# The last feed-forward projection and the final norm, token-major instead of feature-major

## The chip, the cores and the metric

The kernel runs on one core of a Trainium2 chip. The metric is the device time of one execution in microseconds (us), as the median of several runs.

## What is computed

The reference is a decoder trunk of two layers over 512 tokens of 1024 features, all in float32. Each layer mixes tokens in three gated branches (spatial gating, sliding-window attention, gated delta rule), adds the merged result through an output projection, and then adds a SwiGLU feed-forward part. A last RMSNorm follows. What the change touches is the end:

```
x = x + merged @ w_out[layer]
h2 = rmsnorm(x, ffn_norm[layer])
gu = h2 @ w_gate_up[layer]                      # 2 x 2816 columns
x = x + (silu(gu[:, :2816]) * gu[:, 2816:]) @ w_down[layer]
...
out = x * rsqrt(mean(x * x, over features) + 1e-6) * final_norm
```

## The kernel before

**Layout.** Activations are feature-major: a tile holds 128 features on the partitions and all 512 tokens along them, so x is KT = 8 tiles, and the feed-forward activation is KF = 22 tiles. Every matmul is done in three parts, because float32 values are split into a high and a low half (`H` and `L` in the names): high by high, high by low, low by high. In the feature-major projections (`fm_acc`, `fm_tile`) a 128x128 piece of the weight is loaded into TensorE and 512 tokens of an activation stream past it, into one PSUM bank. Some projections are token-major (`tm_group`, among them the z projection `z_proj`): there a 128x128 piece of the activation is loaded, for a chunk of 128 tokens, and 512 columns of weight stream.

**Weights** come through `wload`: one DMA on SP into a staging tile `st` (two buffers), a cast on ScalarE to the high half `wh`, and a subtraction on VectorE to the low half `wl` (three buffers each). These carry a high priority, so they run ahead of the matmuls as buffers allow.

**Order.** A planner (`Issue`) with estimated costs writes the order of TensorE's instructions; streams hand over to each other with `yield`. The other engines and the DMA queues are ordered by the framework's scheduler, by readiness and place in the program. The order on each engine and queue is thus fixed before the run.

**PSUM.** Four banks with the tag `mm` serve the projections, four with the tag `px` the small products.

**Output projection of a layer.** For each m of 8 tiles: 24 matmuls, then the residual tile `xt` is read from DRAM (SP), added on VectorE, written back to `xscr` (SP), and passed to `Norm.add`, which makes the halves `hH` (ScalarE) and `hL` (VectorE) of x times the norm's gain, the square `sq` (ScalarE), and the sum of squares (GpSimd or VectorE). `xt` and `sq` share a pool of five buffers with the tag `rot`.

**Feed-forward part.** 44 tiles of gate and up projection (`wg`), of which the 22 activations are made and split (`aH`, `aL`); then for each m of 8 tiles 22 x 3 = 66 matmuls with `wd`, the residual `xf` and `Norm.add`. In the last layer `Norm.add` squares, sums and multiplies by the final gain. `Norm.finish` then turns the sum of squares into a per-token factor: matmuls with a column of ones, the power -0.5 on GpSimd, a diagonal tile `dg`, a matmul that spreads it over the partitions, and a copy to `rep`. All eight tiles are multiplied by `rep` and written out.

Of the kernel before, what the change touches and what calls it, by code (L numbers as in the profile page):

```python
# [10 lines left out]
F32 = mybir.dt.float32  # L11
# [25 lines left out]
LAT = 0.7  # L37
DMA_LAT = 2.5
DENSE = 10
PAD = 72  # L40
ORDER = "k z qv0 qv1 aq gv u"


# [5 lines left out]
class Issue:  # L49
# [50 lines left out]
    def bank(self, tag, n, t):  # L100
        self.ready[t.tensor.name] = self.bank_free(tag, n)
        self.banks[tag].append(t.tensor.name)
        return t
# [57 lines left out]

@with_exitstack
def hybrid_kernel(ctx, tc, x0, pos, wi, wkv, wb, wo, wg, wd, gn, convw, lngb, sguw, sgub,
                  sinks, alog, dtb, dnn, out, depth=DEPTH):
    issue = Issue()
    nc = issue.front(tc.nc)
    PSUM = bass.MemoryType.PSUM
# [10 lines left out]
    def nm(s):  # L178
        uid[0] += 1
        return f"{s}_{uid[0]}"  # L180
# [7 lines left out]
    def rot(name):  # L188
        return base.tile([P, T], F32, tag="rot", name=nm(name), bufs=N_ROT)
# [7 lines left out]
    def cst(shape, name, dt=F32):  # L197
        return const.tile(shape, dt, name=name, tag=name)
# [15 lines left out]

    xp = tc.tile_pool(name="x0", bufs=1, reuse_waits="tile")
    x0p = xp.__enter__()
    gnt = cst([P, 2 * DEPTH + 1, KT], "gnt")
    cst([P, PAD], "pad")
    nc.sync.dma_start(gnt, gn)
    xin, kv0 = [], []  # L220
# [133 lines left out]
    def split_hl(k):  # L354
        return (base.tile([P, T], F32R, tag=f"hH{k}", name=nm("hH")),
                base.tile([P, T], F32R, tag=f"hL{k}", name=nm("hL")))

    class Norm:


        def __init__(self, gi, final=False, split=KT - 1):

            self.gi = gi
            self.final = final
            self.split = split
            self.accs = []
            self.xs = []

        def add(self, k, xt):
            g = gnt[:, self.gi, k:k + 1]  # L370
            if not self.final:
                xh, xl = split_hl(k)
                nc.scalar.activation(xh, xt, AF.Copy, scale=g)
                nc.vector.scalar_tensor_tensor(xl, xt, g, xh.bitcast(F32), ALU.mult, ALU.subtract)
                self.xs.append((xh, xl))
            sq = rot("sq")
            nc.scalar.activation(sq, xt, AF.Square)
            if k == 0 or k == self.split < KT - 1:
                self.accs.append(sq)
            else:  # L380
                eng = nc.gpsimd if k < self.split else nc.vector
                eng.tensor_tensor(self.accs[-1], self.accs[-1], sq, ALU.add)
            if k == KT - 1 and len(self.accs) > 1:
                nc.vector.tensor_tensor(self.accs[0], self.accs[0], self.accs[1], ALU.add)
            if self.final:
                nc.gpsimd.tensor_scalar(xt, xt, g, 1.0, ALU.mult, ALU.mult)

        def finish(self):
            ps = bank("px")
# [17 lines left out]
            yield  # L407

    xscr = dram.tile([KT, P, T], F32, name="xscr")


    def layer(l, norm, first=None):
# [694 lines left out]

        nx = Norm(2 * l + 1)
        xold = x0 if l == 0 else xscr
        for m in range(KT):  # L1110
            ps = yield from fm_tile(wo[l, m], ms_)
            xt = rot("xt")
            nc.sync.dma_start(xt, xold[m])
            nc.vector.tensor_tensor(xt, ps, xt, ALU.add)
            nc.sync.dma_start(xscr[m], xt)
            nx.add(m, xt)
        mix.__exit__(None, None, None)


        last = l == depth - 1  # L1120
        with tc.tile_pool(name=f"ffn{l}", bufs=1, reuse_waits="tile") as fp:
            hx = nx.xs
            issue.spawn(0, nx.finish(), nx.accs[0])
            act = []
            for i in range(KF):
                pgt = yield from fm_tile(wg[l, 2 * i], hx)
                pup = yield from fm_tile(wg[l, 2 * i + 1], hx)
                if i == 0:
                    yield f"rep{nx.gi}"
                    rep2 = nx.rep  # L1130
                s = rot("s")
                nc.vector.tensor_tensor(s, pgt, rep2, ALU.mult)
                nc.scalar.activation(s, s, AF.Silu)
                nc.gpsimd.tensor_tensor(s, s, rep2, ALU.mult)
                nc.vector.tensor_tensor(s, pup, s, ALU.mult)
                ah = fp.tile([P, T], F32R, tag=f"aH{i}", name=nm("aH"))
                al_ = fp.tile([P, T], F32R, tag=f"aL{i}", name=nm("aL"))
                nc.scalar.copy(ah, s)
                nc.gpsimd.tensor_tensor(al_, s, ah.bitcast(F32), ALU.subtract)
                act.append((ah, al_))  # L1140
            nn = Norm(2 * DEPTH if last else 2 * l + 2, final=last)
            xf = []
            for m in range(KT):
                pd = mm_bank()
                for j, (k0, k1) in enumerate(((0, 8), (8, 16), (16, 22))):
                    w = wload(wd[l, m, :, k0 * P:k1 * P], (k1 - k0) * P)
                    yield from fm_acc(pd, w, 0, act[k0:k1], j == 0, j == 2)
                if last:
                    xt = fp.tile([P, T], F32, tag=f"xf{m}", name=nm("xf"))
                else:  # L1150
                    xt = rot("xt")
                nc.sync.dma_start(xt, xscr[m])
                nc.vector.tensor_tensor(xt, pd, xt, ALU.add)
                if not last:
                    nc.sync.dma_start(xscr[m], xt)
                nn.add(m, xt)
                xf.append(xt)
            if last:
                yield from nn.finish()
                for m in range(KT):  # L1160
                    eng = nc.gpsimd if m in (2, 5) else nc.vector
                    eng.tensor_tensor(xf[m], xf[m], nn.rep, ALU.mult)
                    nc.sync.dma_start(out[m], xf[m])
        return nn

    norm = Norm(0, split=4)
    for k in range(KT):
# [14 lines left out]
def _tiles_fm(w):  # L1182

    K, C = w.shape
    return w.reshape(K // P, P, C // P, P).transpose(2, 1, 0, 3).reshape(C // P, P, K)
# [8 lines left out]
def _rep(a):  # L1194
    return np.ascontiguousarray(np.broadcast_to(a[..., None, :], a.shape[:-1] + (P,) + a.shape[-1:]))


def _layout(x, positions, attn_norm, w_in, sgu_ln_g, sgu_ln_b, sgu_w, sgu_b, attn_sinks, dn_conv_w, dn_a_log,
            dn_dt_bias, dn_norm, w_branch, w_out, ffn_norm, w_gate_up, w_down, final_norm):
    L = w_in.shape[0]  # L1200
    cuts = np.cumsum([0, 512, 512, 512, 128, 128, 1536, 512, 4, 4, 3072])
    perm = np.concatenate([np.arange(h * 64, (h + 1) * 64) for h in HEAD_PERM])
    wi, wkv, wb, wg, wd, wo = [], [], [], [], [], []
    for l in range(L):
        u, v, q, k, vb, qkv, z, be, a, gt = [w_in[l][:, cuts[i]:cuts[i + 1]] for i in range(10)]
        wi.append(np.concatenate([_tiles_fm(qkv), _tiles_fm(u), _tiles_tm(q[:, perm]), _tiles_tm(v), _tiles_tm(z),
                                  _tiles_fm(gt)]))
        wkv.append(_tiles_tm(np.concatenate([k, vb, be, a], axis=1)))
        br = []
        for i in range(3):  # L1210
            w = w_branch[l, i][perm] if i == 1 else w_branch[l, i]
            t = _tiles_fm(w)
            br.append(t.reshape(4, 2, P, 512).transpose(0, 2, 1, 3).reshape(4, P, 1024))
        wb.append(np.stack(br))
        wo.append(_tiles_fm(w_out[l]))
        g = _tiles_fm(w_gate_up[l])
        wg.append(np.stack([g[:KF], g[KF:]], axis=1).reshape(2 * KF, P, 1024))
        wd.append(_tiles_fm(w_down[l]))
    gn = np.concatenate([np.stack([attn_norm, ffn_norm], axis=1).reshape(2 * L, D), final_norm[None]])
    return {  # L1220
        "x0": x[0].T.reshape(KT, P, T),
        "pos": positions[0].reshape(NCH, P).T,
        "wi": np.stack(wi), "wkv": np.stack(wkv), "wb": np.stack(wb), "wo": np.stack(wo), "wg": np.stack(wg),
        "wd": np.stack(wd),
        "gn": gn.reshape(2 * L + 1, KT, P).transpose(2, 0, 1),
        "convw": dn_conv_w.reshape(L, 4, 12, P).transpose(0, 3, 2, 1),
        "lngb": np.concatenate([sgu_ln_g, sgu_ln_b], axis=1).reshape(L, 8, P).transpose(0, 2, 1),
        "sguw": sgu_w.transpose(0, 3, 1, 2),
        "sgub": _rep(sgu_b.reshape(L, 512)).reshape(L, P, 4, P),
        "sinks": _rep(attn_sinks[:, HEAD_PERM]),  # L1230
        "alog": _rep(dn_a_log), "dtb": _rep(dn_dt_bias), "dnn": _rep(dn_norm),
    }


_ORDER = ["x0", "pos", "wi", "wkv", "wb", "wo", "wg", "wd", "gn", "convw", "lngb", "sguw", "sgub", "sinks",
          "alog", "dtb", "dnn"]


# [17 lines left out]
```

## Time and profile before

| | us |
|---|---|
| median of 3 runs | 1779.11 (1778.96 to 1779.59) |
| the profiled execution | 1778.7 |
| its span, first to last instruction | 1776.7 |

The profiled execution's own time is 2.0 us more than its span. All rows of the trace belong to this one execution; times in them count from the start of its span. The granted clock of TensorE is 0.995 of full speed over the span. A row of the timeline gives start, duration, engine, line, operation, out<-in, shapes and, in brackets, how long the engine sat idle before and what ended it. Nearly all instructions carry line 118, that of the helper through which they are issued, so groups are told apart by the names of tiles.

### The profile page before, as it was taken

To read this page: it belongs to the slowest core of one execution; us is meant where nothing else is said; L and a number is where in the kernel's file an instruction comes from. 1 tells how busy PE (TensorE), PEld (TensorE's weight loads), DVE (VectorE), ACT (ScalarE), POOL (GpSimd) and SP (SyncE) were. 2 spreads that over 40 slices of the span, in tenths; PEclk is the share of its full clock that TensorE was granted. 3 is DMA by queue.
4 is the path that set the end of the run, shared out by engine and by line. 5 is a ranking of instruction groups with operands and counts; after the bars stand their busy time and mean duration, and the time that the engine had idled before them with its cause. 6 is when DMAs were issued, how large, how long until landed. Compare 5 with 4: busy or idle time off the path is not lost.

```text
span 1776.7 us, 22123 instructions
## 1 busy us (share of the span) xinstructions
PE 1747.9 (98%) x8458; PEld 1451.2 (82%) x8458; DVE 885.9 (50%) x1756; ACT 633.8 (36%) x1155; POOL 397.3 (22%) x399
## 2 busy tenths in 40 slices
PE   8999999999999999999999999999999999999996
PEld 6888888888888888888888878888888888888885
DVE  7695775444543333333367858644444433333222
ACT  6455454322333222322244435533233332222221
POOL 4413111011223333310043121010222233333111
PEclk9999999999999999999999999999999999999998
DMA  4222112222352232234332311122234522233331
GB/s 158 96 99 73 37 36 78 95 87 103 103 176 95 99 101 97 95 125 128 112 105 98 102 48 37 54 84 90 89 103 134 196 95 95 95 100 99 96 94 62
DMA packets 55784, 171.84 MB, mean 97 GB/s; under 512 B 8000, under 2 KB 8256, under 8 KB 55680
## 3 DMA queue, kind: packets, MB, share of 16 engines
q1 hardware_dynamic: 54432, 167.04, 28.7%
q0 software_dynamic: 1248, 3.41, 0.6%
q8 instruction: 66, 1.08, 0.2%
q14 instruction: 38, 0.31, 0.1%
HBM read 159.41 MB, written 11.01 MB: 96 GB/s over the span
## 4 chain that ended last, share of the span: by engine, by line
PE 96%; DVE 2%; ACT 1%; issue 0%; POOL 0%; DMA 0%; DVEq 0%; SPq 0%; POOLq 0%; ACTq 0%
PE mm L118 86%; PE px L118 10%; DVE wl L118 0%; DVE xf L118 0%; DVE U L118 0%; DMA st<-in_wkv 0%; ACT wh L118 0%; POOL of L118 0%; DVE zg L118 0%; DVE sq L118 0%; DVE Tm L118 0%; DVE ys L118 0%; ACT hH L118 0%; ACT pr L118 0%; ACT sq L118 0%
## 5 line engine op out<-in xcount | busy, mean ns | idle before, releaser
L118 ACT CAST wh<-st 128x1024 fp32r<-128x1024 f32 (+2 forms) x288 | 296.1, 1028 | 794.9 <-PE mm L118 716.0
L118 PE MATMUL mm<-hH,wh 128*128 128x512 f32 x1344 | 532.2, 396 | 0.0
L118 PE MATMUL mm<-hH,wl 128*128 128x512 f32 x1344 | 524.0, 390 | 0.0
L118 PE MATMUL mm<-hL,wh 128*128 128x512 f32 x1344 | 523.3, 389 | 0.0
L118 DVE TENSOR_TENSOR wl<-st,wh 128x1024 fp32r<-128x1024 f32 (+2 forms) x288 | 355.0, 1233 | 184.4 <-ACT wh L118 173.9
L118 PEld LDWEIGHTS mm<-hH,wh 128*128 128x128 f32 x1344 | 252.6, 188 | 52.9 <-issue 3.0
L118 PEld LDWEIGHTS mm<-hH,wl 128*128 128x128 f32 x1344 | 252.2, 188 | 53.1
L118 PEld LDWEIGHTS mm<-hL,wh 128*128 128x128 f32 x1344 | 252.6, 188 | 50.9 <-issue 0.8
L118 PE MATMUL mm<-aH,wh 128*128 128x512 f32 x352 | 136.9, 389 | 0.0
L118 PE MATMUL mm<-aL,wh 128*128 128x512 f32 x352 | 136.9, 389 | 0.0
L118 PE MATMUL mm<-aH,wl 128*128 128x512 f32 x352 | 136.9, 389 | 0.0
L118 POOL TENSOR_TENSOR gt<-gt,gt 128x512 f32<-128x512 f32 x32 | 48.8, 1524 | 301.1 <-DVE gt L118 301.1
L118 POOL TENSOR_TENSOR s<-s,rep 128x512 f32<-128x512 f32 x44 | 77.4, 1759 | 161.6 <-ACT s L118 161.6
L118 POOL TENSOR_TENSOR aL<-s,aH 128x512 fp32r<-128x512 f32 x44 | 76.5, 1739 | 157.4 <-ACT aH L118 157.4
L118 PE MATMUL mm<-wh,hH 128*128 128x512 f32 (+1 forms) x256 | 102.0, 399 | 7.0 <-ACT hH L118 7.0
L118 DVE TENSOR_TENSOR s<-mm,s 128x512 f32<-128x512 f32 x44 | 30.4, 692 | 149.6 <-PE mm L118 142.8
L118 DVE TENSOR_TENSOR s<-mm,rep 128x512 f32<-128x512 f32 x44 | 30.4, 692 | 137.8 <-PE mm L118 133.9
L118 PE MATMUL mm<-wh,hL 128*128 128x512 f32 (+1 forms) x256 | 95.7, 374 | 0.2 <-DVE hL L118 0.2
L118 PE MATMUL mm<-wl,hH 128*128 128x512 f32 (+1 forms) x256 | 94.9, 371 | 0.0
L118 POOL TENSOR_TENSOR sq<-sq,sq 128x512 f32<-128x512 f32 x27 | 40.7, 1507 | 235.9 <-ACT sq L118 235.9
L118 DVE TENSOR_TENSOR gt<-mm,rep 128x512 f32<-128x512 f32 x48 | 33.1, 690 | 98.4 <-PE mm L118 98.4
L118 PEld LDWEIGHTS mm<-aH,wh 128*128 128x128 f32 x352 | 66.1, 188 | 13.8
(250 smaller groups left out, 2359.0 us busy)
## 6 DMA issues: line engine op xcount, KB each, us to landing
st<-in_wi SPq DMA_DIRECT2D x104, 512.0 KB, 3.2
st<-in_wg SPq DMA_DIRECT2D x88, 512.0 KB, 3.3
st<-in_wd SPq DMA_DIRECT2D x32, 512.0 KB, 3.5
st<-in_wb SPq DMA_DIRECT2D x24, 512.0 KB, 3.2
st<-in_wo SPq DMA_DIRECT2D x16, 512.0 KB, 3.3
xscr<-xt SPq DMA_DIRECT2D x24, 256.0 KB, 2.0
st<-in_wd SPq DMA_DIRECT2D x16, 384.0 KB, 3.1
xt<-xscr SPq DMA_DIRECT2D x16, 256.0 KB, 2.8
```

The costliest lines, as they stand in the source:

```text
L118: return f(*args, **kw)
```

## The change

The final layer's down projection is done by a new function, `last_down`, token-major: its accumulators are four chunks of 128 tokens by two halves of 512 features, all eight PSUM banks (four `mm`, four `px`). The weight `wt` is read as 22 tiles of 128 rows by 1024 columns. For the first 19 tiles, each tile is used for all four chunks in turn. The last three tiles are held together, and each chunk takes them one after another, so that the chunks end one by one, 18 matmuls apart. Behind each chunk the residual is added, the squares are summed along the free dimension by ScalarE's accumulator, and the power, the gain (`gft`, the same row on all partitions) and the factor are applied; one half leaves through SP, the other through ScalarE's own DMA queue.

For this x must lie token-major in DRAM. In the last layer's output projection the write to `xscr` is replaced: VectorE transposes the tile `xt` in 32x32 blocks into `xb` (a third user of the `rot` buffers), and four DMAs on SP write it to `xtok`, 32 partitions each, in runs of 32 floats. `last_down` reads `xtok` back as four tiles of 128 tokens.

The branch for the final norm goes from `Norm`, the final gain leaves the tile `gnt`, and the constant `PAD` becomes smaller. On the host the weight and gain are laid out for this, and the output is no longer transposed there.

```diff
--- before.py
+++ after.py
@@ -37,7 +37,7 @@
 LAT = 0.7
 DMA_LAT = 2.5
 DENSE = 10
-PAD = 72
+PAD = 48
 ORDER = "k z qv0 qv1 aq gv u"
 
 
@@ -161,7 +161,7 @@
 
 @with_exitstack
 def hybrid_kernel(ctx, tc, x0, pos, wi, wkv, wb, wo, wg, wd, gn, convw, lngb, sguw, sgub,
-                  sinks, alog, dtb, dnn, out, depth=DEPTH):
+                  sinks, alog, dtb, dnn, wt, gf, out, depth=DEPTH):
     issue = Issue()
     nc = issue.front(tc.nc)
     PSUM = bass.MemoryType.PSUM
@@ -214,7 +214,7 @@
 
     xp = tc.tile_pool(name="x0", bufs=1, reuse_waits="tile")
     x0p = xp.__enter__()
-    gnt = cst([P, 2 * DEPTH + 1, KT], "gnt")
+    gnt = cst([P, 2 * DEPTH, KT], "gnt")
     cst([P, PAD], "pad")
     nc.sync.dma_start(gnt, gn)
     xin, kv0 = [], []
@@ -358,21 +358,19 @@
     class Norm:
 
 
-        def __init__(self, gi, final=False, split=KT - 1):
+        def __init__(self, gi, split=KT - 1):
 
             self.gi = gi
-            self.final = final
             self.split = split
             self.accs = []
             self.xs = []
 
         def add(self, k, xt):
             g = gnt[:, self.gi, k:k + 1]
-            if not self.final:
-                xh, xl = split_hl(k)
-                nc.scalar.activation(xh, xt, AF.Copy, scale=g)
-                nc.vector.scalar_tensor_tensor(xl, xt, g, xh.bitcast(F32), ALU.mult, ALU.subtract)
-                self.xs.append((xh, xl))
+            xh, xl = split_hl(k)
+            nc.scalar.activation(xh, xt, AF.Copy, scale=g)
+            nc.vector.scalar_tensor_tensor(xl, xt, g, xh.bitcast(F32), ALU.mult, ALU.subtract)
+            self.xs.append((xh, xl))
             sq = rot("sq")
             nc.scalar.activation(sq, xt, AF.Square)
             if k == 0 or k == self.split < KT - 1:
@@ -382,8 +380,6 @@
                 eng.tensor_tensor(self.accs[-1], self.accs[-1], sq, ALU.add)
             if k == KT - 1 and len(self.accs) > 1:
                 nc.vector.tensor_tensor(self.accs[0], self.accs[0], self.accs[1], ALU.add)
-            if self.final:
-                nc.gpsimd.tensor_scalar(xt, xt, g, 1.0, ALU.mult, ALU.mult)
 
         def finish(self):
             ps = bank("px")
@@ -407,6 +403,8 @@
             yield
 
     xscr = dram.tile([KT, P, T], F32, name="xscr")
+
+    xtok = dram.tile([T, D], F32, name="xtok")
 
 
     def layer(l, norm, first=None):
@@ -1107,17 +1105,24 @@
 
         nx = Norm(2 * l + 1)
         xold = x0 if l == 0 else xscr
+        last = l == depth - 1
         for m in range(KT):
             ps = yield from fm_tile(wo[l, m], ms_)
             xt = rot("xt")
             nc.sync.dma_start(xt, xold[m])
             nc.vector.tensor_tensor(xt, ps, xt, ALU.add)
-            nc.sync.dma_start(xscr[m], xt)
+            if last:
+                xb = rot("xb")
+                nc.vector.transpose(xb, xt)
+                for a in range(4):
+                    nc.sync.dma_start(xtok.rearrange("(b i) d -> i b d", i=32)[:, :, m * P + 32 * a:m * P + 32 * a + 32],
+                                      xb[32 * a:32 * a + 32, :].rearrange("i (b j) -> i b j", j=32))
+            else:
+                nc.sync.dma_start(xscr[m], xt)
             nx.add(m, xt)
         mix.__exit__(None, None, None)
 
 
-        last = l == depth - 1
         with tc.tile_pool(name=f"ffn{l}", bufs=1, reuse_waits="tile") as fp:
             hx = nx.xs
             issue.spawn(0, nx.finish(), nx.accs[0])
@@ -1138,30 +1143,72 @@
                 nc.scalar.copy(ah, s)
                 nc.gpsimd.tensor_tensor(al_, s, ah.bitcast(F32), ALU.subtract)
                 act.append((ah, al_))
-            nn = Norm(2 * DEPTH if last else 2 * l + 2, final=last)
-            xf = []
+            if last:
+                yield from last_down(fp, act)
+                return None
+            nn = Norm(2 * l + 2)
             for m in range(KT):
                 pd = mm_bank()
                 for j, (k0, k1) in enumerate(((0, 8), (8, 16), (16, 22))):
                     w = wload(wd[l, m, :, k0 * P:k1 * P], (k1 - k0) * P)
                     yield from fm_acc(pd, w, 0, act[k0:k1], j == 0, j == 2)
-                if last:
-                    xt = fp.tile([P, T], F32, tag=f"xf{m}", name=nm("xf"))
-                else:
-                    xt = rot("xt")
+                xt = rot("xt")
                 nc.sync.dma_start(xt, xscr[m])
                 nc.vector.tensor_tensor(xt, pd, xt, ALU.add)
-                if not last:
-                    nc.sync.dma_start(xscr[m], xt)
+                nc.sync.dma_start(xscr[m], xt)
                 nn.add(m, xt)
-                xf.append(xt)
-            if last:
-                yield from nn.finish()
-                for m in range(KT):
-                    eng = nc.gpsimd if m in (2, 5) else nc.vector
-                    eng.tensor_tensor(xf[m], xf[m], nn.rep, ALU.mult)
-                    nc.sync.dma_start(out[m], xf[m])
         return nn
+
+    def last_down(fp, act):
+
+        xs_, fin = [], []
+        gft = fp.tile([P, D], F32, name="gft")
+        nc.sync.dma_start(gft, gf)
+        for c in range(NCH):
+            xt = fp.tile([P, D], F32, tag=f"xf{c}", name=nm("xf"))
+            nc.sync.dma_start(xt, xtok[c * P:(c + 1) * P, :])
+            xs_.append(xt)
+        yield issue.bank_free("mm", 1)
+        banks = [(mm_bank(), bank("px")) for c in range(NCH)]
+
+        def mms(c, k, w):
+            (ah, al_), (wh, wl) = act[k], w
+            tk = slice(c * P, (c + 1) * P)
+            for h in range(2):
+                sl = slice(h * 512, (h + 1) * 512)
+                o = banks[c][h]
+                nc.tensor.matmul(o, lhsT=ah[:, tk], rhs=wh[:, sl], start=k == 0, stop=False)
+                nc.tensor.matmul(o, lhsT=ah[:, tk], rhs=wl[:, sl], start=False, stop=False)
+                nc.tensor.matmul(o, lhsT=al_[:, tk], rhs=wh[:, sl], start=False, stop=k == KF - 1)
+
+        for k in range(KF - 3):
+            w = wload(wt[k])
+            for c in range(NCH):
+                mms(c, k, w)
+                yield
+        ws = [wload(wt[k]) for k in range(KF - 3, KF)]
+        for c in range(NCH):
+            for k in range(KF - 3, KF):
+                mms(c, k, ws[k - KF + 3])
+                yield
+            xt = xs_[c]
+            ss = lay.tile([P, 2], F32, tag="fss", name=nm("fss"), bufs=2)
+            for h in range(2):
+                sl = slice(h * 512, (h + 1) * 512)
+                nc.vector.tensor_tensor(xt[:, sl], banks[c][h], xt[:, sl], ALU.add)
+                sq = rot("sq")
+                nc.scalar.activation(sq, xt[:, sl], AF.Square, accum_out=ss[:, h:h + 1])
+            ms = lay.tile([P, 1], F32, tag="fms", name=nm("fms"), bufs=2)
+            nc.vector.tensor_tensor(ms, ss[:, 0:1], ss[:, 1:2], ALU.add)
+            nc.vector.tensor_scalar(ms, ms, 1.0 / D, EPS, ALU.mult, ALU.add)
+            nc.gpsimd.tensor_tensor(ms, ms, nhalf[:, 0:1], ALU.pow)
+            for h in range(2):
+                sl = slice(h * 512, (h + 1) * 512)
+                nc.vector.tensor_tensor(xt[:, sl], xt[:, sl], gft[:, sl], ALU.mult)
+            nc.vector.tensor_scalar(xt[:, :512], xt[:, :512], ms, None, ALU.mult)
+            nc.sync.dma_start(out[c, :, :512], xt[:, :512])
+            nc.scalar.activation(xt[:, 512:], xt[:, 512:], AF.Copy, scale=ms)
+            nc.scalar.dma_start(out[c, :, 512:], xt[:, 512:])
 
     norm = Norm(0, split=4)
     for k in range(KT):
@@ -1215,25 +1262,27 @@
...
-        wd.append(_tiles_fm(w_down[l]))
...
+        if l < L - 1:
+            wd.append(_tiles_fm(w_down[l]))
...
+        "wt": w_down[L - 1].reshape(KF, P, D), "gf": _rep(final_norm),
...
-    out = nc.dram_tensor("out", (KT, P, T), F32, kind="ExternalOutput").ap()
+    out = nc.dram_tensor("out", (NCH, P, D), F32, kind="ExternalOutput").ap()
...
-    return np.ascontiguousarray(o.reshape(D, T).T)[None]
+    return np.ascontiguousarray(o.reshape(T, D))[None]
```

## Rows read from the trace of the kernel before

**Rows 1.** The page: busy time by engine, and the chain by engine.

```profile
PE 1747.9 (98%) x8458; PEld 1451.2 (82%) x8458; DVE 885.9 (50%) x1756; ACT 633.8 (36%) x1155; POOL 397.3 (22%) x399
...
PE 96%; DVE 2%; ACT 1%; issue 0%; POOL 0%; DMA 0%; DVEq 0%; SPq 0%; POOLq 0%; ACTq 0%
```

**Rows 2.** Timeline of all engines behind the last matmul.

```profile
1757.94 0.39 PE L118 MATMUL mm<-aH,wl 128*128 128x512 f32 x1
1758.37 0.69 DVE L118 TENSOR_TENSOR xf<-mm,xf 128x512 f32<-128x512 f32 x1 [13.36 <-PE mm L118]
1759.15 0.63 ACT L118 ACTIVATE sq<-xf 128x512 f32<-128x512 f32 x1 [14.32 <-DVE xf L118]
...
1762.16 1.02 POOL L118 TENSOR_TENSOR rst<-ms,nhalf 128x4 f32<-128x4 f32 x1 [1.09 <-DVE ms L118]
```

**Rows 3.** The tile `out`: instructions, durations in ns, first and last start.

```profile
L118 SPq DMA_DIRECT2D out<-xf x8: 332/402/462, 1768.6 to 1772.8; - x8
```

**Rows 4.** Timeline of TensorE, z projection and tile m=7 of the last projection.

```profile
942.09 0.48 PE L118 MATMUL mm<-wh,hH 128*128 128x512 f32 x1
...
942.87 0.39 PE L118 MATMUL mm<-wh,hH 128*128 128x512 f32 x1
...
947.40 0.39 PE L118 MATMUL mm<-wh,hL 128*128 128x512 f32 x1
...
1743.21 0.39 PE L118 MATMUL mm<-aH,wh 128*128 128x512 f32 x1
```

**Rows 5.** Timeline of ScalarE and VectorE, a weight split in the last projection.

```profile
1739.15 1.05 ACT L118 CAST wh<-st 128x1024 fp32r<-128x1024 f32 x1 [4.39 <-PE mm L118]
...
1740.23 1.23 DVE L118 TENSOR_TENSOR wl<-st,wh 128x1024 fp32r<-128x1024 f32 x1 [4.22 <-ACT wh L118]
```

**Rows 6.** Groups by form: count, busy us, mean ns, idle before and releaser.

```profile
L118 DVE STREAM_TRANSPOSE U<-Tm 128x128 f32<-128x128 f32 x32 | 8.0, 286 | 0.1
...
L118 DVE TENSOR_SCALAR gv<-gv,mv,rs 128x512 f32<-128x512 f32 x8 | 4.4, 546 | 1.6 <-POOL rs L118 1.3
...
L118 DVE TENSOR_SCALAR rs<-mv 128x1 f32<-128x1 f32 x8 | 1.1, 146 | 0.0
...
L118 ACT ACTIVATE cv<-pre,cw 128x512 f32<-128x512 f32 x24 | 17.3, 722 | 14.4 <-DVE pre L118 14.3
...
L118 ACT ACTIVATION_READ_ACCUMULATOR ojk<-U 128x1 f32 x32 | 6.0, 189 | 0.0
...
L118 POOL DMA_DIRECT2D cols<-sc x4 | 4.7, 1166 | 4.3 <-DMA sc<-nx 2.4 <-DMA sc<-tb 1.9
...
L118 POOL TENSOR_TENSOR rs<-rs,nhalf 128x1 f32<-128x1 f32 x8 | 4.4, 560 | 9.7 <-DVE rs L118 9.7
...
L118 POOL DMA_DIRECT2D sc<-tb x2 | 1.1, 571 | 56.1 <-DVE ssq L118 28.2 <-DVE tb L118 28.0
```

**Rows 7.** Timeline of SP, output projection of layer 1 and behind it.

```profile
1376.49 0.32 SPq L118 DMA_DIRECT2D xscr<-xt  x1
1376.87 0.42 SPq L118 DMA_DIRECT2D xt<-xscr  x1
...
1399.97 2.42 SPq L118 DMA_DIRECT2D xf<-xscr  x5
```

**Rows 8.** DMA issues: KB each, median us from issue to landing.

```profile
xt<-xscr SPq DMA_DIRECT2D x16, 256.0 KB, 2.8
...
cols<-sc POOLq DMA_DIRECT2D x4, 128.0 KB, 3.8
```

**Rows 9.** Timeline of VectorE and TensorE, end of the output projection, layer 1.

```profile
1397.53 0.69 DVE L118 TENSOR_TENSOR xt<-mm,xt 128x512 f32<-128x512 f32 x1 [2.75 <-PE mm L118]
1398.34 1.22 DVE L118 TENSOR_TENSOR wl<-st,wh 128x1024 fp32r<-128x1024 f32 x1
1399.48 0.74 DVE L118 SCALAR_TENSOR_TENSOR hL<-xt,gnt,hH 128x512 fp32r<-128x512 f32 x1
...
1402.27 0.39 PE L118 MATMUL mm<-hL,wh 128*128 128x512 f32 x1
```

More of the change, by code (lines that the diff above doesn't have):

```diff
@@ L1217, in _layout @@
         wg.append(np.stack([g[:KF], g[KF:]], axis=1).reshape(2 * KF, P, 1024))
-        wd.append(_tiles_fm(w_down[l]))
-    gn = np.concatenate([np.stack([attn_norm, ffn_norm], axis=1).reshape(2 * L, D), final_norm[None]])
+        if l < L - 1:
+            wd.append(_tiles_fm(w_down[l]))
+    gn = np.stack([attn_norm, ffn_norm], axis=1).reshape(2 * L, D)
     return {
@@ L1224, in _layout @@
         "wd": np.stack(wd),
-        "gn": gn.reshape(2 * L + 1, KT, P).transpose(2, 0, 1),
+        "gn": gn.reshape(2 * L, KT, P).transpose(2, 0, 1),
         "convw": dn_conv_w.reshape(L, 4, 12, P).transpose(0, 3, 2, 1),
@@ L1235 @@
 _ORDER = ["x0", "pos", "wi", "wkv", "wb", "wo", "wg", "wd", "gn", "convw", "lngb", "sguw", "sgub", "sinks",
-          "alog", "dtb", "dnn"]
+          "alog", "dtb", "dnn", "wt", "gf"]
 def kernel(**inputs):
```

## The prediction

> **What bounds the kernel now.** I read the page first, then the timeline of the stages that the diff touches, engine by engine, and last the groups by form for the price of each operation. The page says that TensorE is busy 98% of the span and 96% of the chain that ended last [rows 1]: nothing off TensorE matters unless TensorE waits for it, or it stands behind the last matmul. So there are two places to look: this tail, and every place where the change could make TensorE wait.
>
> **The tail before.** The last matmul starts at 1757.94 and the span ends at 1776.70: 18.76 us. In it stand, one after another, the addition of the residual, the square, the sum over feature tiles, four small matmuls, the power, the spread by a diagonal and a matmul, its copy `rep`, and only then eight multiplications and eight output transfers [rows 2]. The statistic of a token needs all eight feature tiles, so nothing can leave before the last matmul. The last output transfer is issued at 1772.8 [rows 3], and the span ends 3.9 us later.
>
> **Matmuls: no change.** Before, 8 tiles x 22 x 3 = 528 matmuls of 512 columns; after, 22 x 4 chunks x 2 halves x 3 = 528 of 512 columns. Only the roles change: activations become the loaded operand. In tile m=7 of the last projection, the 65 steps from 1743.21 to 1757.94 are 0.2266 us each; in the token-major z projection, which has the roles of the changed code, the 20 steps from 942.87 to 947.40 are 0.2265 [rows 2, 4]. I take 0. Upper bound: the 23 steps from 942.09, which begin behind small matmuls, are 0.2309 each, and 528 x 0.0043 = 2.3 us. A gain is excluded, since TensorE is back to back already.
>
> **Weights: hidden.** 22 loads of 1024 columns take the place of 16 of 1024 and 8 of 768, the same number of elements. The tight place is the end: there are three split buffers, and the three last tiles are all held at once, so tile 21 can be split only when the last matmul of tile 18 is done. Call the start of that matmul T. A cast starts 0.25 us after the start of the matmul that frees its buffer (1739.15, against 19 steps ahead of 1743.21, which is 1738.90), and cast and difference are done 2.31 later [rows 4, 5]: T+2.56. Tile 21's difference is first read by the 14th matmul behind T, at T+3.17. Cover 0.6 us, cost 0; without it the overrun itself, a microsecond at most. At the start of the stage the bank of the last up-projection is wanted by chunk 3 only 18 matmuls (4 us) on, against an evacuation of 0.69.
>
> **The new tail.** All times from the start L of the last matmul. Chunk 3's first half ends three matmuls before the second; from a matmul's start to VectorE's I take the old 0.43, an addition costs 0.69, a square 0.63 [rows 2]; reading the accumulator 0.19, a small tensor-scalar 0.15, the power of one column 0.56, the scaling 0.55 on VectorE and 0.72 on ScalarE [rows 6]. Addition 0 ends at L+0.44, addition 1 at 1.15. Square 0 with its read ends at 1.36, square 1 at 2.20. The mean's two small operations: 2.26 to 2.57. Power: 2.65 to 3.21. The two multiplications by the gain (0.69 each) fit into VectorE's waits, the first behind square 0, the second beside the power, until 3.26. Scaling ends at 3.83 on VectorE, 4.06 on ScalarE. Then, as before, 0.2 to the issue and 3.9 to the end: L+8.2. The tail gives 18.76 - 8.2 = 10.6 us. Bounds: 9.1, with the power at its four-column price of 1.02 [rows 2] and the multiplications in the way; 11.0, with a little of the scaling hidden. Earlier chunks keep pace: VectorE needs 4 x 0.69 + 0.3 + 0.55 = 3.6 us a chunk, TensorE 18 x 0.2266 = 4.1.
>
> **The price, in the output projection of layer 1 (1357 to 1400).** Each of eight tiles gains a 128x512 transpose, and four writes of 64 KB where one of 256 KB was. The transpose takes 0.286 at 128 columns [rows 6]; for 512 the bounds are 0.29 and four times that, 1.14, and I take the middle, 0.71. In a period of 24 x 0.2266 = 5.44 VectorE has 2.66 of work there (addition, difference, `hL` [rows 9]), so as busy time it is free. As a delay it is not, because of SP's order. In seven of seven cases the load of tile m+1's residual is issued directly behind tile m's write [rows 7], so only one is ever ahead. With four writes in between there is a loop from addition to addition: addition 0.69, transpose 0.71, four issues, the load, which lands 2.8 after its issue [rows 8], and 0.11 of gaps: 4.31 and the issues. A lone issue and the next stand 0.38 apart, issues back to back 0.48 (five in 2.42) [rows 7]: 0.38 + 3 x 0.47 = 1.79. Loop 6.10 against 5.44: each tile slips by 0.66, seven tiles by 4.6. The last `hL` is ready at 1400.22 and first read at 1402.27 [rows 9]; of these 2.05 the transpose takes 0.71, some 1.3 remain. TensorE waits 4.6 - 1.3 = 3.3 us. Bounds: 0, if the load goes ahead of the writes; 16.4, if a write cut into short runs costs SP twice a plain one, as on POOL (1166 against 571 ns [rows 6]): four for 3.66, loop 7.97, 7 x 2.53 - 1.3. I take 3.3: SP's issue times hardly change with what is sent (0.32 to 0.48 in [rows 7]), and that is the nearest row.
>
> The writes consist of 128-byte runs. POOL's gather of `cols`, 128 KB in 2048 runs of 64 bytes, lands in 3.8 us, the residual's plain load in 2.8 [rows 8]: dearer, but not by a factor; for the load behind the writes I take no more than its 2.8, and the rest is a rival below. The Trainium skill, "DMA: Bandwidth & Descriptors", Specifications, speaks against this change: line rate wants at least 512 B, below that the engine reads, modifies and writes. By that rule the load behind the writes would land later and the loop slip more; the `cols` row agrees in direction, but is no write of 128 bytes, and no run yet shows the rule itself.
>
> The loads of four chunks and the gain (2.5 MB where 2 MB were) must await the last write and may stand before weight loads of the up-projections. Five such loads stood in a row before [rows 7], and the chain shows no gap there; I take 0. Without that cover, one stall of 1 to 4 us.
>
> **Sum.** 1778.7 (the profiled execution: span 1776.7 and 2.0 around it) - 10.6 + 3.3 = 1771.4. The median of the runs is 0.4 above that execution: 1771.8.
>
> **Rivals.** Times include the 0.4.
> *The load goes first.* For it: only the buffer holds the load, and that can come free about when the transpose ends. Against: seven of seven behind the write, and the writes come earlier in the program. No wait: 1768.5. Chance 0.28.
> *The weight's difference gets between addition and transpose.* It starts 0.12 us behind the addition and takes 1.22 [rows 9]. The loop is then 7.33, the wait 7 x 1.89 - 1.3 = 11.9: 1780.4, no change. Against: at the addition's end the transpose is ready and the cast is not quite. Chance 0.10.
> *Short runs hold up the load.* Four writes have 2048 runs, as `cols` has; with its 1.0 us more in the loop (7.10) the wait is 7 x 1.66 - 1.3 = 10.3: 1778.8. Against: the writes' data can move while SP is still issuing. Chance 0.09.
> *The other side: issue of the cut writes.* If each keeps SP 0.97 (0.47 x 1166/571), four without any cheap first one, the loop is 8.19, the wait 17.9, the time 1786.4. From 0.71 a write the gain is gone, from 0.84 the kernel is slower by over 0.2%. For it: the POOL rows. Against: SP's even times. Chance 0.07.
> *The tail gains little*, because the chunks' ends queue up: each chunk late adds 4 us, two leave 10.6 - 8 - 3.3, about 1779.8. Against: 3.6 of 4.1. Chance 0.04.
> The forecast keeps 0.42.
>
> **Numbers.** The forecast's own range is 1769 to 1774.5 (waits of 1 to 5 us, tail 9.1 to 11). The range for 8 in 10 begins at the first rival with the tail's 11.0 (1768.1) and half a microsecond for what I priced too dear, 1767.5, and reaches to the short runs, 1779.0. A measurement tells about 0.2%, 3.6 us, from no change, so faster is below 1775.5: forecast, first rival, and the milder half of the short runs and the tail, 0.76. No change 0.16, slower 0.08.
>
> **What will show it.** In the timeline: the last matmul some 8 us before the end, no small matmuls behind it, outputs from two queues, steps of 0.2266 throughout. On SP in the output projection: the order of four writes and one load, their distance; on VectorE additions that drift from 5.44 apart to about 6.1; on TensorE a wait for `hL` near 1402. I am wrong if TensorE waits elsewhere, in the last three weight tiles or the first chunk, or if the additions keep to 5.44.

## The result, and the profile after

The changed kernel takes 1790.03 us (median of 4 runs, 1787.71 to 1792.08), the kernel before 1779.03 in the runs beside it. The ratio is 1.0061, with a 95% interval of 1.0043 to 1.0078: slower by 0.6%, where 1771.8 and a gain were forecast. The profiled execution took 1791.28, with a span of 1789.6, which is 12.9 more than the span before.

The page of the changed kernel hardly shows it. These are its busy times and the granted clock in 40 slices:

```profile
PE 1753.6 (98%) x8448; PEld 1454.2 (81%) x8448; DVE 892.8 (50%) x1773; ACT 636.6 (36%) x1164; POOL 380.6 (21%) x386
...
PEclk9999999999999999999999999999999799999999
```

TensorE is busy 98% of the span, as before [rows 1]. One slice stands out, the 32nd (1387 to 1432 us), with a granted clock of 7 of 10.

**The tail did what it should.** The timeline of all engines behind the last matmul:

```profile
1781.26 0.39 PE L118 MATMUL px<-wh,aL 128*128 128x512 f32 x1
...
1781.69 0.69 DVE L118 TENSOR_TENSOR xf<-px,xf 128x512 f32<-128x512 f32 x1
...
1784.14 0.54 POOL L118 TENSOR_TENSOR fms<-fms,nhalf 128x1 f32<-128x1 f32 x1 [3.54 <-DVE fms L118]
...
1784.72 0.49 DVE L118 TENSOR_SCALAR xf<-xf,fms 128x512 f32<-128x512 f32 x1 [0.72 <-POOL fms L118]
1785.47 0.34 ACTq L118 DMA_DIRECT2D out<-xf  x1
```

From the start of the last matmul to the end of the span it is 1789.6 - 1781.26 = 8.34 us, where it was 18.76 [rows 2]: 10.4 gained. But the last matmul starts 1781.26 - 1757.94 = 23.3 us later than before. The two together are the 12.9.

**Where the 23.3 went.** The waits of TensorE from 1340 to the end (total, times, longest) are only these:

```profile
PE mm L118 <- ACT hH L118: 11.3, 2, 6.9
PE mm L118 <- DVE xt L118: 2.9, 1, 2.9
```

All three stand in the output projection of layer 1 or right behind it. SP's queue there (SPq are DMAs that SP issues, `st` weight loads, x the number of issues in a row):

```profile
1360.49 0.33 SPq L118 DMA_DIRECT2D xtok<-xb  x1
1361.59 0.35 SPq L118 DMA_DIRECT2D st<-in_wo  x1
1361.98 0.97 SPq L118 DMA_DIRECT2D xtok<-xb  x2
1367.04 0.35 SPq L118 DMA_DIRECT2D st<-in_wo  x1
1367.43 0.97 SPq L118 DMA_DIRECT2D xtok<-xb  x2
1372.02 0.35 SPq L118 DMA_DIRECT2D st<-in_wo  x1
1372.41 1.59 SPq L118 DMA_DIRECT2D xtok<-xb  x3
1377.46 0.35 SPq L118 DMA_DIRECT2D st<-in_wg  x1
1377.85 0.43 SPq L118 DMA_DIRECT2D xt<-xscr  x1
```

The load in the last row is the residual of tile 2; that of tile 1 had gone out at 1356.06. It stands behind all eight writes of tiles 0 and 1, and between these stand weight loads (`st`), one per period of 5.44 us. What each waits for is in the same kernel's list of SP's waits, 1355 to 1440:

```profile
SPq L118 <- DVE wl L118: 38.2, 11, 5.2
SPq L118 <- DVE xb L118: 15.3, 7, 4.0
SPq L118 <- DMA xtok<-xb: 5.1, 2, 3.1
```

A weight load waits until VectorE has read its staging buffer (first row), and everything behind it in the queue waits too. So in the rows above two or three DMAs get past per period, and each tile needs five. The last row holds the one place where the shared buffers show here: the load of tile 6 (1408.61) waits 2.0 us for a buffer that a write is still reading; the other 3.1 are a chunk's read behind the last write. VectorE's timeline shows what that does to the additions:

```profile
1364.46 0.69 DVE L118 TENSOR_TENSOR xt<-mm,xt 128x512 f32<-128x512 f32 x1 [2.24 <-PE mm L118]
...
1381.64 1.23 DVE L118 TENSOR_TENSOR wl<-st,wh 128x1024 fp32r<-128x1024 f32 x1 [4.22 <-ACT wh L118]
1382.79 0.68 DVE L118 TENSOR_TENSOR xt<-mm,xt 128x512 f32<-128x512 f32 x1
...
1410.63 0.69 DVE L118 TENSOR_TENSOR xt<-mm,xt 128x512 f32<-128x512 f32 x1 [6.64 <-DMA xt<-xscr]
...
1419.22 0.69 DVE L118 TENSOR_TENSOR xt<-mm,xt 128x512 f32<-128x512 f32 x1 [4.21 <-DMA xt<-xscr]
```

The additions (`xt<-mm,xt`) are those of tiles 1, 2, 5 and 7. Between the first two lie 18.3 us instead of 5.44. VectorE's own order adds a little: the loads of tiles 2 and 3 land at 1381.3 and 1392.8 (3.4 and 3.5 us after their issue), but each addition stands behind a weight's difference (`wl`), and starts 1.5 and 0.9 us later.

For the longest wait, 6.9 us, the chain of work that ended last (start, duration, what) shows the whole path:

```profile
1402.76 1.24 DVE wl L118
...
1405.41 5.12 DMA xt<-xscr
...
1410.63 0.70 DVE xt L118
```

The weight's difference frees a staging buffer, SP issues the weight load at 1404.01, then two writes, then at 1405.41 the load of tile 5, and the addition follows as soon as that has landed.

**Waits of 14.2 us cost 23.** Most of the rest is the clock. TensorE's timeline behind the last wait, and the window from 1400 to 1425 (its length, then busy time and count of TensorE, its weight loads, VectorE, ScalarE and GpSimd, then granted clock, DMA share, GB/s):

```profile
1425.08 0.63 PE L118 MATMUL mm<-hH,wl 128*128 128x512 f32 x1
1425.51 0.63 PE L118 MATMUL mm<-hH,wh 128*128 128x512 f32 x1
```

```profile
1400.00:1425.00 25.00, 13.55 (x43) 9.02 (x42) 8.88 (x13) 6.15 (x9) 4.44 (x4) 0.69 0.47 113
```

Steps are 0.43 us there instead of 0.2266: the lower of the two levels, 1.2 GHz. By an estimate from the steps between 1391 and 1431, slow matmuls cost some 7 us; another 2 come with steps of 0.77 to 0.79 between 1412 and 1421.5, in which TensorE waits for the next `hL` or `hH` without a row in the list. Slow matmuls count as busy, which is why the page still says 98%.

### The profile page after: what moved, and what is told of

It is laid out like the page before. It is cut to its first block, busy times and chain, and to the rows that moved or that the text cites. A ratio compares the mean times of both kernels' runs of the same rounds, so it can differ in the third digit from the quotient of the medians.

```text
span 1789.6 us, 22119 instructions
## 1 busy us (share of the span) xinstructions
PE 1753.6 (98%) x8448; PEld 1454.2 (81%) x8448; DVE 892.8 (50%) x1773; ACT 636.6 (36%) x1164; POOL 380.6 (21%) x386
## 4 chain that ended last, share of the span: by engine, by line
PE 95%; DVE 2%; ACT 1%; DMA 1%; issue 1%; SPq 0%; POOL 0%; POOLq 0%; DVEq 0%; ACTq 0%
PE mm L118 81%; PE px L118 14%; DMA xt<-xscr 0%; DVE wl L118 0%; ACT wh L118 0%; SPq L118 0%; DVE U L118 0%; DMA st<-in_wkv 0%; DVE zg L118 0%; POOL of L118 0%; DVE xt L118 0%; ACT hH L118 0%; DVE sq L118 0%; DVE hL L118 0%; DVE ys L118 0%
## 5 line engine op out<-in xcount | busy, mean ns | idle before, releaser
L118 PE MATMUL mm<-brH,wh 128*128 128x512 f32 x192 | 74.7, 389 | 0.0
L118 PE MATMUL mm<-brL,wh 128*128 128x512 f32 x192 | 74.7, 389 | 0.0
L118 PE MATMUL mm<-brH,wl 128*128 128x512 f32 x192 | 74.7, 389 | 0.0
L118 POOL TENSOR_TENSOR sq<-sq,sq 128x512 f32<-128x512 f32 x21 | 30.6, 1459 | 179.8 <-ACT sq L118 179.8
L118 PE MATMUL mm<-aH,wh 128*128 128x512 f32 x176 | 68.5, 389 | 0.0
```

The costliest lines, as they stand in the source:

```text
L118: return f(*args, **kw)
```

## The experiments

Three theories. *Queue*: residual loads stand behind writes and waiting weight loads on SP. *Buffers*: the transposed tile is a third user of the five shared `rot` buffers, and keeps them from loads and squares. *Runs*: pieces of 128 bytes are slow wherever they stand. The runs of the kernel before beside those below have medians of 1778.68 to 1778.91; the ratios are to these.

**The writes on GpSimd's queue.**

```diff
-                    nc.sync.dma_start(xtok.rearrange(...
+                    nc.gpsimd.dma_start(xtok.rearrange(...
```

> The 32 writes of the transposed tiles are issued from GpSimd's queue and not from SP's; nothing else differs from the changed kernel (1790 us). Queue theory: on SP the writes and residual loads stand behind weight loads that wait for a staging buffer, so with the writes gone from SP the residual loads come in time again and the 23 us lost around the output projection return: 1768 to 1772, with the last few us depending on how GpSimd's four issues and its sum of squares fit into 5.44 us a tile. Buffer theory (xb as third user of five shared buffers makes the residual loads late): no change, 1785 to 1792. Run theory (the 128-byte runs are slow to move): at best a little, 1780 to 1790.

Measured: 1779.45 (ratio 1.0002, 0.9991 to 1.0013). The changed kernel stands 22.5 us above the version with one plain write per tile (1767.56, below); about half of that, 10.6 us, came back. The time is in none of the three ranges. SP's timeline now has no writes in it, and still the load of tile 2 comes late; the second fence is from the list of SP's waits:

```profile
1361.92 5.77 SPq L118 DMA_DIRECT2D st<-in_wo  x2
1368.07 0.33 SPq L118 DMA_DIRECT2D xt<-xscr  x1
```

```profile
SPq L118 <- DVE hL L118: 8.1, 5, 2.4
```

The load stands behind two weight loads, and in five cases SP waits for a shared buffer that `hL` has to read first. The Trainium skill, "DMA: Bandwidth & Descriptors", section "Issuing engines are not separate DMA queues", says that issuing from several engines saves only the sequencer's issue time. Here the second queue gained 10.6 us. All 32 issues on SP take about 32 x 0.48 = 15 us, so by its size the gain could be issue time. The run at 1768.43 us below speaks against that: it leaves all 32 issues on SP and gets 21.6 us back. What the second queue saved is then standing behind another transfer's wait, which that rule leaves out.

**The transposed tile in four buffers of its own, writes on SP.**

```diff
...
-                xb = rot("xb")
+                xb = xpool.tile([P, T], F32, tag="xb", name=nm("xb"), bufs=4)
```

> The transposed tile xb gets four buffers of its own, so the shared five are used by xt and sq alone, as before the change; the 32 writes stay on SP. Buffer theory: 1768 to 1772, residual loads in time. Queue theory: nothing comes back, 1785 to 1792, because weight loads still stand between the writes on SP. Run theory: the same, 1785 to 1792.

Measured: 1788.85 (1.0056, 1.0034 to 1.0079). TensorE still waits 9.8 and 2.9 us, and the first 18 us of SP's queue have the order shown above. Freeing buffers that way alone leaves the loss.

**One write of 256 KB per tile, and four writes of long rows.** Both leave the transposed tile in block order in DRAM, so the residual that is read back is misarranged.

```diff
+    xlin = xtok.rearrange("t d -> (t d)").rearrange("(m p n) -> m p n", m=KT, n=T)
...
-                for a in range(4):
-                    nc.sync.dma_start(xtok.rearrange(...
+                nc.sync.dma_start(xlin[m], xb)
```

```diff
...
                 for a in range(4):
-                    nc.sync.dma_start(xtok.rearrange(...
+                    nc.sync.dma_start(xlin[m, 32 * a:32 * a + 32, :], xb[32 * a:32 * a + 32, :])
```

> Each transposed tile is written with one DMA of 256 KB in long rows of 2 KB, to places that do not match the read behind it, so the residual that is added at the end is wrongly arranged; all else is as in the changed kernel, with the transpose and the five shared buffers. Queue theory: one write per tile as before the change, 1768 to 1770. Run theory: the same, 1768 to 1770. Buffer theory: xb still takes one of the five buffers, 1775 to 1790.

> Four writes per tile from SP as in the changed kernel, but each of 32 rows of 2 KB and not of 512 runs of 128 bytes; they go to places that do not match the read behind it, so the residual that is added at the end is wrongly arranged. Run theory: 1768 to 1771. Queue theory: four writes still stand among weight loads on SP, 1778 to 1792. Buffer theory: 1780 to 1792.

Measured: 1767.56 (0.9936, 0.9914 to 0.9959) for one write, with additions 5.44 apart and no wait of TensorE; 1779.53 (1.0004, 0.9993 to 1.0016) for four long ones. So four writes instead of one cost 12 us even in long rows. The other 10.5 us to the changed kernel come with the short runs, though a long-run write lands only 0.2 us sooner (2.4 against 2.6). The order on SP differs too. With four long writes more get past a weight load, as its timeline shows:

```profile
1361.45 0.34 SPq L118 DMA_DIRECT2D st<-in_wo  x1
1361.83 4.71 SPq L118 DMA_DIRECT2D xtok<-xb  x5
1366.88 0.35 SPq L118 DMA_DIRECT2D st<-in_wo  x1
1367.28 0.90 SPq L118 DMA_DIRECT2D xtok<-xb  x2
1368.28 0.37 SPq L118 DMA_DIRECT2D xt<-xscr  x1
```

Tile 2's load goes out at 1368.3, not 1377.9. That order is fixed by the scheduler before the run, so this pair does not tell the runs from the order; the next experiments change the order with the short runs kept.

**Eight buffers for the residual tiles, short writes on SP.**

```diff
...
-            xt = rot("xt")
+            xt = xpool.tile([P, T], F32, tag="xt", name=nm("xt"), bufs=8) if last else rot("xt")
```

> The eight residual tiles of the last output projection get eight buffers of their own, so that no residual load waits for a shared buffer; the 32 short-run writes stay on SP. If what costs is that the residual arrives late (its load stands in SP's queue behind weight loads and writes), all eight loads now stand ahead of the first write, the additions keep to 5.44 us apart and the time is 1767 to 1770. If it is the writes themselves (SP's queue full with 32 issues, so that weight loads come late), TensorE waits for weights instead of for hH, and the time stays at 1778 or above. If the transpose or the writes' buffer cost something on VectorE, the additions drift although the loads are early: 1772 to 1778.

Measured: 1772.95 (0.9965, 0.9952 to 0.9978). The loads are ahead of the first write and the additions 5.44 apart, as the first branch says, but the time is 3 us above its range. One wait is left, for the sum of squares. Rows of the timelines of ScalarE, VectorE and TensorE, in this order:

```profile
1403.56 0.63 ACT L118 ACTIVATE sq<-xt 128x512 f32<-128x512 f32 x1 [0.28 <-DMA xtok<-xb]
1403.31 1.23 DVE L118 TENSOR_TENSOR wl<-st,wh 128x1024 fp32r<-128x1024 f32 x1 [1.71 <-ACT wh L118]
1404.45 0.69 DVE L118 TENSOR_TENSOR sq<-sq,sq 128x512 f32<-128x512 f32 x1
...
1405.28 1.10 PE L118 MATMUL px<-ones,sq 128*128 128x1 f32 x8 [2.90 <-DVE sq L118]
```

The last square had to wait 0.28 us for a shared buffer that a write was still reading. But it ends at 1404.19, and the sum starts at 1404.45, straight behind a weight's difference that had itself waited for ScalarE's cast. So what sets the sum's start is its place in VectorE's order.

**Writes on GpSimd and four buffers of its own for the transposed tile.** The two edits above at once.

> Both halves at once: the 32 writes are issued by GpSimd's queue, and the transposed tile has four buffers of its own. If SP's queue and the shared buffers together are the whole loss, nothing is left between a residual load and its addition, and the time is 1767 to 1771, as with one plain write per tile (1767.6). If GpSimd pays for the issues (2.6 us per tile on an engine that also sums squares there), TensorE still waits at the first up-projection and the time is 1773 to 1779. If writes from GpSimd alone did all that can be had, it stays at 1779.5.

Measured: 1772.34 (0.9967, 0.9954 to 0.9979), between the first two ranges. The additions are 5.44 apart but for one step of 5.50; the one wait left is the 2.9 us for the sum of squares. VectorE's timeline gives its cause:

```profile
1402.68 1.22 DVE L118 TENSOR_TENSOR wl<-st,wh 128x1024 fp32r<-128x1024 f32 x1 [3.03 <-ACT wh L118]
1403.83 0.68 DVE L118 TENSOR_TENSOR sq<-sq,sq 128x512 f32<-128x512 f32 x1
```

GpSimd's last sum ends at 1396.6 and the last square at 1398.4, so it is not GpSimd's issues. VectorE stands idle for 3 us in front of a weight's difference, and the sum is behind that in its order, as in the run before.

**Eight residual buffers, and two for the squares, short writes on SP.**

```diff
...
-            sq = rot("sq")
+            sq = self.sqp() if self.sqp and k else rot("sq")
...
+            nx.sqp = lambda: xpool.tile([P, T], F32, tag="sq", name=nm("sq"), bufs=2)
```

> Eight own buffers for the residual tiles as before, and two own buffers for the squares as well, so that the five shared ones hold only the transposed tiles and one running sum; the 32 short-run writes stay on SP. The version with eight residual buffers alone still lost 2.9 us where TensorE waited for the sum of squares, whose last square had waited for a shared buffer that a write still held, and about 1.7 us in matmuls at half clock behind it. If that was the rest of the loss, no wait of TensorE is left and the time is 1767 to 1769.5, although SP still issues 32 short-run writes late. If the late writes cost something themselves (chunk reads, weight loads of the first up-projections behind them), it stays at 1771 to 1774.

Measured: 1768.43 (0.9941, 0.9926 to 0.9956), with no wait of TensorE. This is the run that decides. The sum of squares now starts at 1401.19, ahead of the next weight's difference (1406.19): the two more buffers changed the order. SP still issues two or three writes per period, and they land later than in the changed kernel (3.6 against 2.6 us); its timeline:

```profile
1378.88 0.35 SPq L118 DMA_DIRECT2D st<-in_wg  x1
1379.28 1.58 SPq L118 DMA_DIRECT2D xtok<-xb  x3
...
1429.67 0.43 SPq L118 DMA_DIRECT2D xtok<-xb  x1
```

The last write goes out at 1429.7, some 30 us after its tile, and TensorE has no wait. Late writes cost nothing here; what cost time in the other runs was a load that stood behind them, or a buffer that they held.

**Residual loads on ScalarE's queue, shared buffers kept.**

```diff
-            nc.sync.dma_start(xt, xold[m])
+            (nc.scalar if last else nc.sync).dma_start(xt, xold[m])
```

> As the changed kernel, with the residual loads of the last output projection issued by ScalarE's queue in place of SP's; the writes stay on SP and the shared buffers stay five. If the order on SP (residual loads behind weight loads and writes) is the cause alone, the additions keep to 5.44 us and the time is 1767 to 1773. If the shared buffers bind as well (SP drains only 2 to 3 of the 4 writes per tile, so transposed tiles keep buffers that loads and squares want), loads and squares still come late, on ScalarE now, and the time is 1776 to 1788.

Measured: 1783.98 (1.0030, 1.0018 to 1.0041). The order on SP is no longer in the loads' way, and most of the loss stays. Rows of its timeline:

```profile
1376.47 0.33 ACTq L118 DMA_DIRECT2D xt<-xscr  x1
1376.89 1.05 ACT L118 CAST wh<-st 128x1024 fp32r<-128x1024 f32 x1 [2.18 <-POOL sq L118]
...
1391.58 0.63 ACT L118 ACTIVATE sq<-xt 128x512 f32<-128x512 f32 x1 [0.85 <-DMA xtok<-xb]
1392.24 0.33 ACTq L118 DMA_DIRECT2D xt<-xscr  x1
...
1396.63 0.69 DVE L118 TENSOR_TENSOR xt<-mm,xt 128x512 f32<-128x512 f32 x1 [4.63 <-DMA xt<-xscr]
```

The load of tile 3, in the first row, goes out when GpSimd's sum has read a square (1376.44), and the cast behind it waits as long. Later a square waits for a buffer that a late write holds, the next load stands behind the square, and the addition starts 4.4 us behind the load's issue. So the shared buffers bind without SP's order, and SP's order binds when the transposed tiles have buffers of their own (1788.85 above).

**The rearrangement in the reads.** One plain write per tile; the chunks are read back by 16 DMAs of 128 KB in runs of 128 bytes, on SP or on GpSimd's queue.

```diff
+                nc.sync.dma_start(xlin[m], xb)
...
-            nc.sync.dma_start(xt, xtok[c * P:(c + 1) * P, :])
+            for b in range(4):
+                nc.sync.dma_start(xt[32 * b:32 * b + 32, :].rearrange("i (n j) -> i n j", j=32),
+                                  xlin.rearrange("m (a i) t -> i (m a) t", i=32)[:, :, c * P + 32 * b:c * P + 32 * b + 32])
```

> The transposed tile is written with one plain DMA of 256 KB, and the rearrangement into tokens is done when the chunks are read back: 16 reads of 128 KB in runs of 32 floats instead of four plain ones, on SP during the up-projections. If the loss is only the four writes in the loop of the output projection, the time is that of the one plain write, 1766 to 1769. If short runs or 16 issues on SP cost wherever they stand, weight loads of the up-projections come late: one or two stalls of 1 to 4 us with half clock behind them, 1770 to 1780.

> As the one before (one plain write per tile, 16 short-run reads), but the reads are issued by GpSimd's queue. If the reads are hidden in either queue, the same time, 1766 to 1769. If SP's queue is the scarce place in the up-projections too, this one is faster than the one before by the stalls there. If GpSimd pays 0.65 us or more for each read, 16 of them take 10 to 20 us from its activation work (one subtraction per tile pair) and the time is 1768 to 1775.

Measured: 1767.71 on SP (0.9940, 0.9925 to 0.9955), 1768.44 on GpSimd (0.9945, 0.9930 to 0.9959); the two can't be told apart. Neither has a wait of TensorE. The window of the SP version that answers to the one above:

```profile
1400.00:1425.00 25.00, 25.00 (x114) 20.44 (x113) 9.17 (x12) 8.30 (x10) 7.45 (x5) 1.00 0.48 125
```

TensorE is busy throughout at full clock. This version does the whole computation and is faster than both kernels.

**Without the staggered end.** The SP version above, with all 22 weight tiles taken through the four chunks in turn.

```diff
-        for k in range(KF - 3):
+        for k in range(KF - 1):
...
-        ws = [wload(wt[k]) for k in range(KF - 3, KF)]
+        ws = [wload(wt[k]) for k in range(KF - 1, KF)]
```

> One plain write per tile and 16 short-run reads on SP (the version that took 1767.7), but the weight tiles go through all four chunks to the end: no three last tiles held together, so the chunks end 6 matmuls (1.36 us) apart instead of 18 (4.08 us). If the staggered ending is what the tail's gain rests on, the chunks' ends queue up on VectorE, which needs 3.6 us for each: four of them end about 14.4 us behind the first addition near L - 4.5, so the tail from the last matmul's start L is 13 to 15 us instead of 8.3, and the time is 1772 to 1775. If token-major alone gives the gain and the chunks' ends overlap anyway, it stays at 1767 to 1769.

Measured: 1773.88 (0.9972, 0.9962 to 0.9982). Rows of its timeline, first addition to last output:

```profile
1753.31 0.69 DVE L118 TENSOR_TENSOR xf<-mm,xf 128x512 f32<-128x512 f32 x1 [9.25 <-PE mm L118]
...
1757.65 0.39 PE L118 MATMUL px<-wh,aL 128*128 128x512 f32 x1
...
1767.99 0.34 ACTq L118 DMA_DIRECT2D out<-xf  x1
```

The tail is 1771.7 - 1757.65 = 14.05 us. The chunks' ends queue up on VectorE. Against 8.2 us with the staggered end, 5.8 us of the gain go: token-major alone is worth 18.76 - 14.05 = 4.7 us, the 18 matmuls between the ends the rest.

## Why the prediction was wrong

**The tail** was right: L+8.2 forecast, 8.34 measured, and 8.2 in the version with rearranged reads. The single prices held too: power 0.54 (0.56 taken), scaling 0.49 on VectorE (0.55) and 0.72 on ScalarE. The rival that the tail gains little fell; the run without the staggered end shows when it would have been true.

**Matmuls and weights** at nothing: right. TensorE has no wait behind the one that ends at 1420.7, and steps in the last three weight tiles are 0.2266.

**Late loads** at nothing: right. Where the residuals are in time, neither four loads of 512 KB nor 16 short-run ones make TensorE wait.

**The price, in the output projection**, is the step that failed, at its first sentence and not in its sizes. The transpose takes 0.71, as taken; a write takes SP 0.48, as taken; the addition 0.69. The loop was built on the premise that tile m+1's load stands directly behind tile m's writes, because it did in seven of seven cases before [rows 7]. The order on a queue belongs to one program. In the changed one the load of tile 2 stands behind eight writes and four weight loads, and each weight load waits for a staging buffer that comes free once in 5.44 us. The working counted SP's time for issues and left out what else waits in SP's queue. So 3.3 us of waits was forecast, and 14.2 came, which with the clock cost 23.3. The waits lie below the upper bound of 16.4, but by luck: that was made from a dearer issue in the same loop, and knew neither the weight loads nor the clock.

A second fault: the third user of the shared buffers got no price. Moving the writes to another queue left 12 us of the loss, against the 1767.6 of one plain write, and own buffers for the transposed tile took 7 of these away. Moving the loads left 16, and there the part of the buffers is read from its timeline alone. A third: waits were priced at their length, and 14.2 us of them brought some 9 more. A fourth, smaller: the loads of tiles 2 to 7 landed in 2.7 to 5.1 us, where 2.8 was taken.

**The rivals.** *The load goes first* had been priced at 1768.5. Made true with eight residual buffers alone it measured 1772.95, because the sum of squares came late; with two more for the squares, 1768.43. Its mechanism was right and it was not what the program did. *Short runs hold up the load*: as a matter of the transfer, no. 32 short-run writes on SP cost 0.9 us against one plain write per tile (1768.43 against 1767.56), and the single times of the two overlap. The loads did land later than taken, but behind four long writes just as late (2.7 to 5.6 us against 2.7 to 5.1). The Trainium skill, "DMA: Bandwidth & Descriptors", Specifications, says that line rate wants at least 512 B, and the prediction weighed this. Little of it shows here: in the changed kernel a write of 128-byte runs landed in 2.6 us, one of long rows in 2.4, and where nothing stands behind the writes, no time is lost. *Issue of the cut writes dear*: the sign came true and the mechanism fell, since the issues cost 0.48, not 0.97. *The weight's difference between addition and transpose*: each of the eight transposes starts 0.71 to 0.80 behind the start of its addition, so nothing got between them. Differences did get in front of the additions of tiles 2 and 3, which cost these 1.5 and 0.9 us (above).

**What stays open.** Why the scheduler sets the short-run writes and the loads of the changed program in just this order isn't in any trace, nor why the loads landed later than before; shown is only that orders without a load behind the writes, with buffers to match, lose nothing.

## What to carry to other kernels

Where a change puts more DMAs on a queue, list everything that stands in that queue in one period and what each entry waits for: a prefetch that waits for its buffer turns all entries behind it into late ones. Don't carry the order of a queue over from the old trace; ask which load would be ruinous if it stood last, and give that one its own buffers, so that it can go first. If data must be rearranged through DRAM, put the many small DMAs on the side that has slack, here the reads, which had the whole up-projection to hide in.

## What was not expected of the hardware

A wait of TensorE costs more than its length: behind waits of 2.9 to 6.9 us the matmuls of 512 columns ran 0.4267 us apart instead of 0.2266, the last time for about 6 us (1424.1 to 1430.2). The granted clock was 0.69 from 1400 to 1425.

Runs of 128 bytes were nearly as quick as long ones at these sizes: in the changed kernel 64 KB in 512 runs landed in 2.6 us, in the version with long rows in 2.4, and SP's issue took 0.48 against 0.42. From GpSimd's queue the same write took 0.65 to issue and landed in 2.9. These are medians of one program each, and the program matters more than the run length: the same short-run writes landed in 3.5 to 3.6 us where the loads had gone ahead or to ScalarE's queue, and in 4.1 from GpSimd with own buffers.
